# Free order for the terms of a sum, a program order chosen by replays with paused loads, paced w_ada rows, c as a column, a halved last sum

## The chip, the cores and the metric

One core of one Trainium2 chip. The metric is the device time of one execution in microseconds (us), and less is better. Before the change the median of 3 runs is 836.93 us (836.46 to 839.16).

## The reference, cut to what matters

Two decoder layers over 256 tokens of width 1024, all in fp32. Each layer is a mixing half and a SwiGLU half, and both are shifted, scaled and gated by rows of `w_ada` against silu(c).

```python
for l in range(2):
    ada = silu(c) @ w_ada[l] + b_ada[l]          # 1024 x 6144
    sh_m, sc_m, g_m, sh_f, sc_f, g_f = split(ada, 6)
    h = rms_norm(x, norm_mix[l]) * (1 + sc_m) + sh_m
    parts = h @ w_in[l]                          # 1024 x 4888 in 12 pieces
    y_a = nsa_mixer(...)                         # sparse attention, with a small MLP over key blocks
    y_b = moba_mixer(...)
    merged = gate_a * (y_a @ w_up_nsa[l]) + gate_b * (y_b @ w_up_moba[l])
    x = x + g_m * (merged @ w_out[l])
    h = rms_norm(x, norm_ffn[l]) * (1 + sc_f) + sh_f
    gt, up = split(h @ w_ffn_in[l], 2)           # 1024 x 5632
    x = x + g_f * ((silu(gt) * up) @ w_ffn_out[l])   # 2816 x 1024
```

## The kernel before, in words

Every weight is read once, in loads of about 1 MB into three buffers called `raw` (128 partitions x 2048 fp32), all from the queue of SyncE (SP, helper `dma`, L563). A loaded unit is mostly *split*: ScalarE (ACT) writes `hi`, the weight rounded to the matmul's fp32r format (L533), and VectorE (DVE) writes `lo = raw - hi` (L485). The activations are kept split in the same way (`hp` with a high and a low part, `mT`, `aT`). A product is then three matmuls into one PSUM bank: high by `hi`, high by `lo`, low by `hi`. `mm3` (L806) issues the three as one burst:

```python
with R.burst():
    mm(o, xh, wh, first, False)
    mm(o, xh, wl, False, False)
    mm(o, xl, wh, False, last)
```

`part` (L812) strings the bursts of a unit over its blocks of 128 rows. A few units are used whole in fp32 (`raw,hd` and `raw,yy` in the trace).

The order of the work on each engine is not written out by hand. The functions of the model record operations in a `Program`; `order()` lists them by a model of costs, buffers and DMA, and the result is emitted as one fixed stream for each engine. In `rounds()` the listing is repeated 40 times; `blame()` raises the rank of whatever the longest idle gaps of the matrix engine (TensorE, PE) were waiting for, and the round with the shortest planned span is kept. Writes into one bank keep the order in which they were recorded. Where the plan has PE idle for 1.4 us or more, `fill()` (L415) puts in dummy matmuls on zeros (`zb`).

The stages: `lead_in` (L1019) takes c, x, the first rows of `w_ada` (tiles `sa`) and the first 1816 columns of `w_in`, one 128-row block k at a time; `sublayer_mix` makes the other columns (`dense`), the block MLP (`mlp`, L1232), both attentions, the two up-projections and `w_out`; `h_chain` turns the new x into the next `hp`; `sublayer_ffn` (L1538) does the SwiGLU half. In the lead, c arrives as a row on one partition; two ACT and two DVE operations of 1x512 make silu(c), and four fp32 matmul passes against `ones` spread it over the partitions (`crow`).

The other rows of `w_ada` come in 80 loads of 0.5 MB into three buffers `aw`. Each is multiplied with `crow` and summed by one DVE operation (`ada_dot`, L491). `ada_pace` spreads their recording among the weight loads; the planner is free to issue them earlier or later than that.

At the end `ffn_out` of layer 1 fills four banks (2 halves of the tokens by 2 halves of the columns); the last unit's terms go round all four, each is multiplied with the gate `gbc` and added to x on DVE (`resid`), and four stores write `out`.

## Time and profile before

| | us |
|---|---|
| median of 3 runs | 836.93 (836.46 to 839.16) |
| the profiled execution | 833.42 |
| span of its trace, first to last instruction | 831.5 |
| PE busy | 810.5 (97%) |
| DVE busy | 578.0 (70%) |
| ACT busy | 419.9 (50%) |
| share of the 16 DMA engines used by loads and stores | 62.9% |

The trace is read as follows. Each engine works through its own list in the order of the program, so a waiting instruction holds up those behind it. A matmul is pipelined: its own time (0.39 us for 512 columns) is longer than the distance to the next one, so "busy" counts some waiting as work, and the distance between two starts is the better measure. A row of the timeline gives start, time, engine, line, operation and, in brackets, how long the engine had been idle and on what. The chain of waits follows back from the last instruction what released each step.

### The profile page before, as it was taken

Reading aid. Unit: us, or ns where it says so; the run is one execution under the profiler, and the core shown is the slowest. Engines: PE = TensorE matmul, PEld = TensorE weight load, DVE = VectorE, ACT = ScalarE, POOL = GpSimd, SP = SyncE. Lnnn points to the kernel's source line nnn. Section 1 sums busy time; section 2 is a strip of 40 time slices with the busy share of each in tenths; the row PEclk is TensorE's granted clock in tenths of the full one; section 3 lists DMA queues with packets and bytes.
Section 4 is the critical chain, followed back from the end, with each engine's and each line's share of the span. In section 5 each row is a group of like instructions: output and inputs, shape, how many; then the busy total and the mean of one; then the engine's idle time right before and its main releaser. Section 6 shows DMA issues by size and latency. Waiting matters only on the chain.

```text
span 831.5 us, 10528 instructions
## 1 busy us (share of the span) xinstructions
PE 810.5 (97%) x3983; PEld 612.0 (74%) x3983; DVE 578.0 (70%) x1014; ACT 419.9 (50%) x667; POOL 66.1 (8%) x69
## 2 busy tenths in 40 slices
PE   9998999999999999999999999999999999999996
PEld 4566756764768887898878877776567888889885
DVE  6878877777787776778778897866378534464443
ACT  6444465861583433444376556587457534443331
POOL 4602610000000000000000313000000000000000
PEclk9999999999999999999999999999999999999999
DMA  9987474449938899887948775540284455465531
GB/s 364 381 302 254 135 263 134 178 158 333 343 121 298 281 304 327 303 308 287 347 153 283 248 239 183 187 151 1 102 294 162 138 189 181 151 203 202 200 104 50
DMA packets 75252, 183.82 MB, mean 221 GB/s; under 512 B 4129, under 2 KB 9265, under 8 KB 75202
## 3 DMA queue, kind: packets, MB, share of 16 engines
q1 hardware_dynamic: 75154, 183.08, 62.9%
q8 instruction: 31, 0.51, 0.3%
q14 instruction: 19, 0.16, 0.1%
q0 software_dynamic: 48, 0.08, 0.0%
HBM read 182.10 MB, written 1.05 MB: 220 GB/s over the span
## 4 chain that ended last, share of the span: by engine, by line
PE 77%; DVE 8%; DMA 8%; ACT 3%; issue 2%; POOL 2%; SPq 0%; DVEq 0%; POOLq 0%; ACTq 0%
PE bank L550 72%; PE bank L555 5%; DVE lo L485 4%; DMA aw<-in_w_ada 2%; DMA raw<-in_w_in 2%; ACT hi L533 2%; DMA rows<-in_rows 1%; DVE tmp L485 1%; DMA raw<-in_w_ffn_in 1%; DMA raw<-in_w_out 1%; POOL tmp L485 1%; DVE tmp L503 1%; POOL tmp L503 1%; DVE aw L491 1%; ACT hp L533 1%
## 5 line engine op out<-in xcount | busy, mean ns | idle before, releaser
L550 PE MATMUL bank<-hi,hp 128*128 128x512 f32 (+2 forms) x1296 | 408.8, 388 | 1.5 <-DVE hp L485 0.7
L485 DVE TENSOR_TENSOR lo<-raw,hi 128x2048 fp32r<-128x2048 f32 (+2 forms) x107 | 243.0, 2286 | 122.6 <-ACT hi L533 122.4
L533 ACT ACTIVATE hi<-raw 128x2048 fp32r<-128x2048 f32 (+2 forms) x107 | 201.7, 1892 | 230.3 <-PE bank L550 173.3
L550 PEld LDWEIGHTS bank<-hi,hp 128*128 128x128 f32 x1296 | 239.3, 189 | 57.0 <-issue 6.5
L550 PE MATMUL bank<-lo,hp 128*128 128x512 f32 (+2 forms) x648 | 244.9, 378 | 4.2 <-DVE lo L485 4.0
L550 PEld LDWEIGHTS bank<-lo,hp 128*128 128x128 f32 x648 | 122.4, 189 | 29.7 <-DVE lo L485 6.9
L491 DVE SCALAR_TENSOR_TENSOR aw<-aw,crow 128x1024 f32<-128x1024 f32 x80 | 95.8, 1219 | 24.6 <-DMA aw<-in_w_ada 24.4
L550 PE MATMUL bank<-hi,aT 128*128 128x512 f32 x352 | 111.9, 392 | 0.0
L550 PEld LDWEIGHTS bank<-hi,aT 128*128 128x128 f32 x352 | 66.1, 188 | 13.4
L550 PE MATMUL bank<-lo,aT 128*128 128x512 f32 x176 | 68.6, 390 | 0.0
L550 PE MATMUL bank<-raw,yy 128*128 128x512 f32 x128 | 58.3, 598 | 0.1
L550 PE MATMUL bank<-raw,hd 128*128 128x512 f32 (+1 forms) x112 | 49.1, 568 | 0.0
L550 PE MATMUL bank<-hi,mT 128*128 128x512 f32 x128 | 43.2, 404 | 0.1
L550 PEld LDWEIGHTS bank<-raw,yy 128*128 128x128 f32 x128 | 23.2, 190 | 26.2 <-issue 23.4
L497 DVE CUSTOM_DVE_ANT_0 at<-bank,maskf 128x128 f32<-128x128 f32 (+1 forms) x96 | 29.2, 352 | 16.6 <-PE bank L555 14.9
L555 PE MATMUL bank<-ident,tmp 128*128 128x128 f32 x256 | 38.6, 282 | 1.1 <-ACT tmp L874 0.4
L555 PEld LDWEIGHTS bank<-ident,tmp 128*128 128x128 f32 x256 | 31.3, 145 | 9.8 <-issue 2.6
L550 PEld LDWEIGHTS bank<-lo,aT 128*128 128x128 f32 x176 | 33.1, 188 | 6.3
L533 ACT ACTIVATE at<-at,nb,rqa 128x128 f32<-128x128 f32 (+1 forms) x64 | 34.2, 536 | 4.4 <-DVE nb L491 4.4
L550 PEld LDWEIGHTS bank<-raw,hd 128*128 128x128 f32 x112 | 20.3, 190 | 16.2 <-issue 14.3
L485 POOL TENSOR_TENSOR tmp<-tmp,tmp 128x512 f32<-128x512 f32 (+1 forms) x9 | 11.7, 1296 | 219.1 <-DVE tmp L491 212.6
L550 PEld LDWEIGHTS bank<-hi,mT 128*128 128x128 f32 x128 | 24.0, 188 | 5.7 <-DVE mT L491 0.6
(183 smaller groups left out, 723.5 us busy)
## 6 DMA issues: line engine op xcount, KB each, us to landing
raw<-in_w_ffn_in SPq DMA_DIRECT2D x44, 1024.0 KB, 5.9
aw<-in_w_ada SPq DMA_DIRECT2D x80, 512.0 KB, 4.8
raw<-in_w_in SPq DMA_DIRECT2D x30, 1024.0 KB, 5.1
raw<-in_w_ffn_out SPq DMA_DIRECT2D x22, 1024.0 KB, 5.2
sa<-in_w_ada SPq DMA_DIRECT2D x8, 1024.0 KB, 10.6
raw<-in_w_out SPq DMA_DIRECT2D x8, 1024.0 KB, 5.6
raw<-in_w_in SPq DMA_DIRECT2D x8, 908.0 KB, 8.5
raw<-in_w_up_nsa SPq DMA_DIRECT2D x4, 1024.0 KB, 5.3
```

The source lines that it names most:

```text
L485: self._vec(engs, cols(out), True, lambda v: v.tensor_tensor(AP(out), AP(a), AP(b), op=op), [a, b], [out])
L491: lambda v: v.scalar_tensor_tensor(AP(out), AP(a), AP(s), AP(b), op0=op0, op1=op1, **{k: AP(x) for k, x in kw.items()}),
L497: lambda v: v.tensor_tensor_reduce(AP(out), AP(a), AP(b), 1.0, init, op0, op1, AP(accum)),
L503: lambda v: v.tensor_scalar(AP(out), AP(a), AP(s1), AP(s2), op0=op0, **kw),
L533: op = self.p.op({"ACT": (c, [lambda: self.nc.scalar.activation(AP(out), AP(a), func, **{k: AP(x) for k, x in kw.items()})])}, reads + lis ...
L550: op = self.p.op({"PE": (cost, [lambda: self.nc.tensor.matmul(AP(out), AP(lhsT), AP(rhs), start=start, stop=stop)])}, [lhsT, rhs], [out])
L555: self.p.op({"PE": (0.109, [lambda: self.nc.tensor.transpose(AP(out), AP(a), AP(ident))])}, [a, ident], [out])
```

## The change

1. **Terms of a sum** (`mm3`, `part`, new `term` and `Sum`): the matmuls that add into one bank no longer have an order among themselves. The planner may place each as soon as its own operands are there; the one that happens to be last closes the sum.
2. **Choosing the order** (`rounds`, new `steps` and `replay`; `blame` is gone): each of 60 listings is replayed 8 times with pauses drawn at random between loads. Waits of PE in these replays raise ranks, and the listing with the shortest mean is kept. Several costs of the model are new (issue of a load 0.43 instead of 0.07 us, doubled PE cost up to 5.4 us, slower POOL, another rule for the number of dummy matmuls).
3. **Rows of w_ada** (`paced`): an `aw` load may be issued only in its recorded turn among the SP loads; the recorded spacing is changed (`ADA_PACE`).
4. **c as a column**: the host hands c as 128x8; the silu is done on 128x8 and eight transposes of broadcast columns spread it. The first `sa` is loaded in two halves.
5. **w1 of the block MLP** is rearranged on the host, so that its load is 128 rows of 2048 contiguous values instead of 128x16 pieces of 128.
6. **The last sum**: in layer 1 the fourth bank is summed in two halves of 256 columns, one after the other; the last unit's terms get ranks by bank; the gate's operations get a rank of 100; the residual and the store of that bank are in halves too.

```diff
+    def term(self, out, lhsT, rhs, first):
+        v = out.val
+        if first:
+            v.sums, v.terms, v.gone = {}, 0, 0
+        s = v.sums.setdefault(out.part, Sum())
+        v.terms += 1
+        def go():
+            v.gone += 1
+            self.nc.tensor.matmul(AP(out), AP(lhsT), AP(rhs), start=first, stop=v.gone == v.terms)
...
-    def mm3(o, xs, wh, wl, first, last):
+    def mm3(o, xs, wh, wl, first):
         xh, xl = xs[:2]
-        with R.burst():
-            mm(o, xh, wh, first, False)
-            mm(o, xh, wl, False, False)
-            mm(o, xl, wh, False, last)
+        E_.term(o, xh, wh, first)
+        E_.term(o, xh, wl, False)
+        E_.term(o, xl, wh, False)
```

```diff
 rounds()
         for i in range(self.ROUNDS):
-            self.order()
-            if best is None or self.span < best[0] - 1e-9:
-                best = (self.span, [op.boost for op in self.ops])
-            to = self.blame()
+            steps = self.steps(self.order())
+            runs = [self.replay(steps, seed) for seed in range(self.RUNS)]
+            span = sum(r[0] for r in runs) / self.RUNS
+            if best is None or span < best[0] - 1e-9:
+                best = (span, [op.boost for op in self.ops])
             for op in self.ops:
-                op.boost += self.WEIGHT * to.get(op.no, 0.0)
+                w = sum(r[1].get(op.no, 0.0) for r in runs) / self.RUNS
+                op.boost = self.FADE * (op.boost - own[op.no]) + own[op.no] + self.WEIGHT * w
 fill()
-        cost, n = self.ZERO, int((t1 - t0 - self.IDLE) / self.ZERO)
-        if t0 < 3.0:
-            cost, n = self.FIRST_ZERO
+        cost = self.ZERO * (2 if t0 < self.COLD else 1)
+        n = int((t1 - t0 - (self.IDLE if t0 > self.START else 0.2)) / cost)
 order()
-                if "SP" in op.alts and op.no != loads[0] and self.ops[loads[0]].stage == "lead":
+                if "SP" in op.alts and op.no != loads[0] and (op.paced or self.ops[loads[0]].stage == "lead"):
                     continue
 ada_rows()
-        dma(aw, A["w_ada"][l, kind * D + k * P:kind * D + (k + 1) * P], late=ada_late)
+        dma(aw, A["w_ada"][l, kind * D + k * P:kind * D + (k + 1) * P]).paced = True
```

```diff
 lead_in()
-        for i in range(2):
-            th = temp()
-            ci = cr[:, i * 512:(i + 1) * 512]
-            act(th[0:1], ci, AF.Tanh, scale=0.5)
-            stt(th[0:1], th[0:1], 1.0, ci, ALU.add, ALU.mult)
-            b = R.val("acc")
-            mm(b, ones, th[0:1], True, True)
+        cg = R.val("ccol")
+        act(cg, cc, AF.Tanh, scale=0.5)
+        stt(cg, cg, 1.0, cc, ALU.add, ALU.mult)
+        for i in range(2):
+            b = R.val("acc")
+            with R.burst():
+                for k in range(4):
+                    tr(b[:, k * P:(k + 1) * P], cg[:, 4 * i + k:4 * i + k + 1].to_broadcast([P, P]), ident)
 sublayer_ffn()
+            parts[(NT - 1, 1)] = [(0, 256), (256, 512)]
+            keys += [(i, t, k, c, e) for t in range(NT) for c in range(2) for e in parts[(t, c)]
+                     for i in range(nu - nl, nu) for k in range(2)]
...
+            R.boost = 20.0 * (4 - 2 * t - c) - e0 / 50 if l == L - 1 and i >= nu - nl else 0.0
+            mm3(b, aT[t][kk], us[i].hi[:, k, cs_], us[i].lo[:, k, cs_], kk == 0)
```

PE's emitted instructions go from 3614 to 3644, DVE's from 916 to 926, ACT's from 559 to 547, POOL's from 74 to 80; the matmuls on `aT` go from 352 and 176 of 512 columns to 340 and 170 of 512 and 24 and 12 of 256.

**Where the change moves instructions.** First SP's queue at the end of the lead: the last block's load (128x1816), the two w1 loads of the block MLP (`in_nsa_cmp_k_w1`, `in_nsa_cmp_v_w1`), rows of `w_ada` (`aw`) and the first `dense` unit (128x4x512). Before:

```order
L563 DMA raw0_473<-in_w_in 128x1816
...
L563 DMA aw1_73<-in_w_ada 128x1024
L563 DMA aw2_74<-in_w_ada 128x1024
L563 DMA aw0_72<-in_w_ada 128x1024
L563 DMA raw1_522<-in_nsa_cmp_k_w1 128x16x128
L563 DMA raw0_528<-in_nsa_cmp_v_w1 128x16x128
L563 DMA aw1_73<-in_w_ada 128x1024
L563 DMA aw2_74<-in_w_ada 128x1024
L563 DMA raw2_555<-in_w_in 128x4x512
```

and with the change:

```order
L678 DMA raw2_485<-in_w_in 128x1816
...
L678 DMA raw2_536<-in_nsa_cmp_k_w1 128x2048
L678 DMA raw1_561<-in_nsa_cmp_v_w1 128x2048
L678 DMA raw0_582<-in_w_in 128x4x512
L678 DMA aw0_72<-in_w_ada 128x1024
L678 DMA raw1_676<-in_w_in 128x4x512
```

Five `aw` loads no longer stand ahead of the first dense unit. Further on, in layer 0's SwiGLU half, the `aw` loads stand singly or by twos and threes between weight loads where they had stood in runs of three to five; one run of five is left.

Second PE at the second unit of layer 0's `w_out`, where `hi` and `lo` are the split unit, `mT` the merged activations, and a bank is one sum. Before:

```order
L550 MATMUL bank_66<-hi_1578,mT_1597 128x512
L550 MATMUL bank_67<-hi_1609,mT_1597 128x512
L550 MATMUL bank_67<-lo_1632,mT_1597 128x512
L550 MATMUL bank_67<-hi_1609,mT_1597 128x512 x2
L550 MATMUL bank_67<-lo_1632,mT_1597 128x512
```

and with the change:

```order
L662 MATMUL bank_67<-hi_1620,mT_1595 128x512 x5
L662 MATMUL bank_66<-hi_1584,mT_1595 128x512 x2
L662 MATMUL bank_67<-hi_1620,mT_1595 128x512
L662 MATMUL bank_66<-lo_1597,mT_1595 128x512
L662 MATMUL bank_67<-hi_1620,mT_1595 128x512
L662 MATMUL bank_66<-hi_1584,mT_1595 128x512
L662 MATMUL bank_67<-lo_1639,mT_1595 128x512 x3
```

One matmul on the unit's `hi` stood ahead of the first on its `lo`; now seven do, with four of the unit before among them.

Third PE in layer 1's `w_ffn_in`, ahead of the second last block of 256 columns (`hi_5354`), with the change:

```order
L662 MATMUL bank_67<-hi_5297,hp_4627 128x256
L669 MATMUL bank_69<-ident_95,tmp_75 128x128 x4
L456 LDWEIGHTS zb_109
L456 MATMUL bank_68<-zb_109 128x512
...
L662 MATMUL bank_65<-hi_5354,hp_4627 128x256
L662 MATMUL bank_65<-lo_5373,hp_4627 128x256
```

Eleven dummy matmuls stand at the mark where rows are left out; before, none stood anywhere in layer 1's SwiGLU half. The other dummies: after the lead 11 before and 4 with the change; ahead of the first real matmul 8 before and none; at the start of layer 0's SwiGLU half 3 and at the boundary of the layers 2 before, none now. Before the x transposes 11 before, and 5 and 18 around the transposes of c now.

## Rows read from the trace of the kernel before

**Rows 1.** The page's part 1: busy time of each engine over the span.

```profile
PE 810.5 (97%) x3983; PEld 612.0 (74%) x3983; DVE 578.0 (70%) x1014; ACT 419.9 (50%) x667; POOL 66.1 (8%) x69
```

**Rows 2.** Stretches of time: busy time by engine, granted clock, DMA share, GB/s.

```profile
61.00:76.00 15.00, 10.93 (x103) 7.83 (x102) 11.73 (x24) 7.46 (x12) 2.28 (x2) 0.89 0.88 319
210.00:225.00 15.00, 13.80 (x67) 11.16 (x66) 12.79 (x13) 8.49 (x7) 1.29 (x1) 1.00 1.00 362
445.00:650.00 205.00, 203.16 (x1085) 149.00 (x1084) 150.06 (x337) 123.69 (x244) 20.62 (x12) 1.00 0.54 181
700.00:750.00 50.00, 50.00 (x236) 41.82 (x235) 24.45 (x16) 19.95 (x15) 0.00 (x0) 1.00 0.56 193
...
70.00:73.00 3.00, 2.54 (x9) 2.12 (x10) 3.00 (x3) 2.08 (x8) 0.00 (x0) 0.60 1.05 406
```

**Rows 3.** The chain of waits around 220: start, time, what, count.

```profile
216.45 8.19 PE bank L550 x36
```

**Rows 4.** Timeline of PE before the first real matmul of the lead.

```profile
11.08 2.64 PE L415 MATMUL bank<-zb 128*128 128x512 bf16 x8
13.56 2.78 PE L550 MATMUL bank<-raw,hd 128*128 128x512 f32 x7
```

**Rows 5.** Timeline of PE in the lead, block k=1.

```profile
32.56 0.50 PE L550 MATMUL bank<-lo,hp 128*128 128x512 f32 x1 [1.08 <-DVE lo L485]
```

**Rows 6.** Timeline of PE between the lead and the first dense unit.

```profile
61.34 2.54 PE L415 MATMUL bank<-zb 128*128 128x512 bf16 x11
64.86 0.23 PE L550 MATMUL bank<-zb,identb 128*128 128x128 bf16 x1 [0.98 <-DVE tmp L485]
...
70.46 0.57 PE L550 MATMUL bank<-sel,at 128*128 128x60 f32 x2 [3.09 <-ACT at L533]
```

**Rows 7.** Timeline of SP's own queue at the end of the lead.

```profile
54.41 3.99 SPq L563 DMA_DIRECT2D aw<-in_w_ada  x2
```

**Rows 8.** The chain of waits after the lead.

```profile
58.51 9.32 DMA raw<-in_w_in
```

**Rows 9.** Timelines of PE, stalls and dummies from 213 to 441.

```profile
213.92 0.50 PE L550 MATMUL bank<-lo,mT 128*128 128x512 f32 x1 [1.20 <-DVE lo L485]
...
241.97 0.82 PE L415 MATMUL bank<-zb 128*128 128x512 bf16 x3
243.24 1.27 PE L555 MATMUL bank<-ident,tmp 128*128 128x128 f32 x8 [0.45 <-ACT tmp L874]
...
247.93 0.50 PE L550 MATMUL bank<-lo,hp 128*128 128x512 f32 x1 [0.42 <-DVE lo L485]
...
319.56 0.50 PE L550 MATMUL bank<-lo,hp 128*128 128x512 f32 x1 [1.50 <-DVE lo L485]
...
432.24 0.61 PE L415 MATMUL bank<-zb 128*128 128x512 bf16 x2
...
434.25 0.73 PE L550 MATMUL bank<-hi,hp 128*128 128x512 f32 x2 [0.38 <-DVE hp L485]
...
440.32 0.40 PE L550 MATMUL bank<-lo,hp 128*128 128x280 f32 x1 [0.96 <-DVE lo L485]
```

**Rows 10.** The chain of waits ahead of the stall at 319.56.

```profile
308.14 7.91 DMA aw<-in_w_ada
```

**Rows 11.** The waits: engine, waited for, us in total, times, longest us.

```profile
DVE aw L491 <- DMA aw<-in_w_ada: 24.4, 11, 5.7
```

**Rows 12.** Timeline of PE over matmuls of 256 columns.

```profile
757.23 0.40 PE L550 MATMUL bank<-hi,hp 128*128 128x256 f32 x2
757.47 0.28 PE L550 MATMUL bank<-lo,hp 128*128 128x256 f32 x1
```

**Rows 13.** Timeline of PE, its last matmul.

```profile
824.49 0.39 PE L550 MATMUL bank<-hi,aT 128*128 128x512 f32 x1
```

**Rows 14.** Timeline of DVE, the last two groups.

```profile
822.92 2.68 DVE L485 TENSOR_TENSOR tmp<-bank,gbc 128x512 f32<-128x512 f32 x4 [8.09 <-PE bank L550]
825.52 2.48 DVE L485 TENSOR_TENSOR x<-x,tmp 128x512 f32<-128x512 f32 x4
```

More of the change, by code (lines that the diff above doesn't have):

```diff
@@ L1 @@
+import random
 from collections import deque
@@ L271, in order @@
         parts = False
+        parked, aside = {}, set()
         def place(op):
             t = 0.0
+            picks = []
+            for v in op.acc:
+                if not v.placed and v not in op.new:
+                    parked.setdefault(id(v), []).append(op)
+                    aside.add(op)
+                    return None
+            if not op.new:
+                return t, picks
             taken = {}
-            picks = []
-            if any(not v.placed for v in op.acc if v not in op.new):
-                return None
             for v in op.new:
@@ L282, in place @@
                 taken[id(k)] = i + 1
-                if len(k.queue) <= i or k.queue[i] is not v:
-                    if sum(not c.busy for s in k.slots for c in s.cells) - i <= LOOSE.get(v.name, 99):
-                        return None
+                if k.queue[i] is not v:
+                    if i == 0:
+                        parked.setdefault(id(v), []).append(op)
+                        aside.add(op)
+                    return None
                 best = None
@@ L419, in fill, with steps @@
         return t0, op
-    def blame(self):
-        to, end = {}, 0.0
-        for op in sorted((o for o in self.ops if o.placed[1] == "PE"), key=lambda o: o.placed[0]):
-            t, e, c = op.placed
-            gap, end = t - end, t + c
-            if gap < 0.25 or t < self.START:
-                continue
-            seen = set()
-            while op is not None and len(seen) < 14 and op.no not in seen:
-                seen.add(op.no)
-                to[op.no] = max(to.get(op.no, 0.0), min(gap, 3.0))
-                ready, by = max(op.waits, key=lambda w: w[0], default=(0.0, None))
-                if by is not None and by.placed[1] == "PE" and len(seen) > 1 and ready < op.placed[0] - 0.3:
+    def steps(self, out):
+        at, used, held, steps = {}, {}, {}, []
+        for i, (_, e, op) in enumerate(out):
+            deps = [at[n] for n in op.preds]
+            for v in op.new:
+                for cell in v.slot.cells:
+                    was = held.get(id(cell))
+                    if was is not None:
+                        deps += used[id(was)].values()
+                    held[id(cell)] = v
+            for v in op.acc:
+                used.setdefault(id(v), {})[e] = i
+            at[op.no] = i
+            steps.append((e, op, op.alts[e][0], [(d, 0.0 if steps[d][0] == e and not steps[d][1].bytes else
+                                                  LAT["SP"] if steps[d][1].bytes else LAT[steps[d][0]]) for d in set(deps)]))
+        return steps
@@ new lines, in replay @@
+    def replay(self, steps, seed):
+        rng = random.Random(seed)
+        free = dict.fromkeys(LAT, 0.7)
+        start, end, by = [], [], []
+        dma, table, parts, gaps = 0.0, (), False, []
+        for i, (e, op, c, deps) in enumerate(steps):
+            ready, who = 0.0, -1
+            for d, lat in deps:
+                if end[d] + lat > ready:
+                    ready, who = end[d] + lat, d
+            idle = free[e]
+            if e == "PE":
+                if op.stage != "fill" and op.parts != parts:
+                    parts = op.parts
+                    idle += self.SWITCH[2]
+                if idle < self.COLD and op.stage != "fill":
+                    c *= 2
+                if ready - idle > 0.25 and ready > self.START:
+                    gaps.append((ready - idle, i))
+            elif e == "ACT":
+                if op.loads is not None:
+                    table = op.loads
+                if op.func is not None and op.func not in table:
+                    table = next(x for x in TABLES if op.func in x)
+                    idle += 1.28
+            t = max(idle, ready)
+            start.append(t)
+            by.append(who)
+            free[e] = t + c
+            if e == "SP":
+                pause = rng.random()
+                if op.stage == "lead" or pause < 0.75:
+                    pause = 0.0
+                else:
+                    pause = 0.6 * rng.random() if pause < 0.9 else 0.6 + rng.expovariate(1.4)
+                dma = max(dma, t + c + 0.1) + op.bytes / 412e3 + pause
+                end.append(dma + 1.9)
+            else:
+                end.append(t + c + (5.1 if op.bytes else 0.0))
+        to = {}
+        for gap, i in gaps:
+            n = 0
+            while i >= 0 and n < 14:
+                no = steps[i][1].no
+                to[no] = max(to.get(no, 0.0), min(gap, 3.0))
+                j, n = by[i], n + 1
+                if j >= 0 and steps[j][0] == "PE" and n > 1 and end[j] < start[i] - 0.5:
```

211 lines of the change are left out of this document (126 added, 85 removed).

## The prediction

> **What bounds the kernel now.** I first read the page's busy times [rows 1]: PE is busy for 97% of the span, every other engine far less, so a microsecond is only won where PE waits, runs dummies or runs at half clock. Busy is not work, though. In a stretch without a wait the chain shows 36 matmuls of 512 columns in 8.19 us [rows 3], so one takes its turn every 0.2275 us, while its own row says about 0.39: a shown idle of PE therefore understates a stall by 0.16 us. Next the table by stretches [rows 2]: 700 to 750, layer 1's SwiGLU half, has PE busy all through and DMA at 0.56, nothing to win. 61 to 76 has PE busy for 10.93 of 15 us at a granted clock of 0.89. 210 to 225 has DMA at 1.00 and 1.2 us of idle PE. Then the timelines of PE, where the reader is to look for brackets and for `zb` rows [rows 4 to 6], [rows 9], and last the chain and SP's queue for what was late [rows 7, 8, 10].
>
> The plan reorders everything, so I price the places where PE loses time now, then what the new order adds. The sum is made against the profiled execution, 833.42 us (span 831.5 and 1.9 around it); that lies 3.5 under the median of the runs, 836.93, and I carry the difference over to that.
>
> **Head and lead.** The first real matmul starts at 13.56, behind eight dummies begun at 11.08 [rows 4], 2.48 us after them. The change drops those dummies, shortens silu(c) (two ACT and two DVE operations of 1x512 become one each of 128x8) and lets the first row sums start on half of the first 1 MB load. The eight added transposes replace four matmul passes. If the loads then set the start, the gain is 0; if the dummies covered all of it, 2.5, and more with the earlier c. In block k=1 PE waits 1.08+0.16 = 1.2 us for `lo` [rows 5]; the new order has five sums' terms on `hi` ahead of it. But the blocks' loads run at the same rate as before and set the end of the lead in part, so I take 2.5 for both, bounds 0.5 and 5.
>
> **After the lead.** This is the largest loss: 11 dummies, 2.54 us; a wait of 0.98; one of 3.09 [rows 6]. At 67.8 the first dense unit lands, issued at 58.51 and 9.32 us on the way [rows 8], and it was issued that late because SP had two `aw` loads in front of it, 3.99 us of its queue [rows 7], with DMA behind them at 0.88 [rows 2]. The new queue has this unit right behind the two w1 loads and ahead of five `aw` loads. Five times 0.5 MB at 319 GB/s [rows 2] is 7.8 us of transfer out of its way; of that the wait for its buffer, freed by the lead's last blocks, takes some back. PE then has dense terms on `hi`, twelve of them placed before the first on `lo`, 2.7 us of work, instead of waiting for the block MLP's chain. Of the losses 2.54+1.14+3.25 = 6.9 and the clock's (below, 1.65), 8.6 in all, four dummies and some wait for the MLP's input remain: I take 6.0, bounds 3.5 and 8.5.
>
> The granted clock is 0.60 in 70 to 73, after the idle of 3.09, and 0.89 over the 15 us [rows 2]; full being 2.4 GHz and half 1.2, 0.11 of 15 us below full means 3.3 us at half clock and 1.65 us lost. The Trainium skill (TensorE: Matmul & The Clock Gate, Part 1) says that throttled is the default and that activity releases it, so an idle matrix engine falls back to 1.2 GHz. The trace agrees here. By that rule fewer dummies in this place are a risk; it is the second rival below.
>
> **w_out and the SwiGLU half of layer 0.** At 213.92 PE waits for `lo` of a unit whose `hi` is there: 1.20+0.16 = 1.36. Three dummies (3 x 0.2275 = 0.68), 0.45+0.16 and 0.42+0.16 follow at the turn to `w_ffn_in` [rows 9]. Together 3.2. Seven matmuls on the unit's `hi` and four of the unit before now stand ahead of its first `lo`, 11 x 0.2275 = 2.5 us against one matmul's 0.23: the cover is 2.3 us longer than the wait. What is late next is the transfer itself, DMA being at 1.00 [rows 2]. I take 2.5, bounds 0.5 and 3.2.
>
> **w_ada rows.** At 319.56 PE waits 1.50+0.16 = 1.66 for a `lo` [rows 9] that stood on DVE behind a row sum waiting 7.91 us on its `aw` load [rows 10]. DVE waits 24.4 us in this way in 11 places [rows 11]; only here does it reach PE at this size. With runs of `aw` loads broken up, I take 1.5, bounds 0 and 1.7. A paced load that is not yet due costs SP nothing in the plan, but one that waits for its buffer on the chip holds the weight loads behind it: that is the third rival.
>
> **Boundary of the layers.** Two dummies (0.46), 0.38+0.16 and 0.96+0.16 [rows 9] make 2.1; no dummies there now, and terms on `hi` to fill. I take 1.6, bounds 0 and 2.1.
>
> **Layer 1's mixing half.** PE is idle for 1.84 of 205 us [rows 2], spread over small waits for POOL and ACT which a free order of terms fills only in part: 1.0, bounds -1 and 1.8.
>
> **Tail.** The last matmul starts at 824.49 [rows 13]; four products and four sums on DVE then end at 828.0 [rows 14], 3.1 us after PE. The four products begin only at 822.92, after 8.09 us of idle, and then run back to back, since the banks are finished nearly together. With the gate ranked early and the banks finished one after another, the last bank's 25 matmuls of 256 columns (0.12 each, [rows 12]) take 3.0 us, in which DVE does the other banks; behind PE's end a product and a sum of 256 columns and what DVE still has queued are left, some 1.25 us by halves of the 0.67 and 0.62 that one takes there. That is 1.85 won. Thirty-six matmuls of 0.12 for eighteen of 0.2275 cost 0.2, one more store in SP's queue 0.2 or so. Net 1.4, bounds 0.7 and 1.8.
>
> **The new dummies.** Eleven `zb` matmuls stand in layer 1's SwiGLU half, where PE now has no gap [rows 2]. They run whether needed or not: 11 x 0.2275 = 2.5 us at least; the plan leaves up to 1.2 of idle beside such a group. I take -2.7, bounds -3.7 and -2.5.
>
> The contiguous w1 loads and the changed costs I put at nothing by themselves: the transfers lie beside the lead's last matmuls; without that cover they are in the 6.0.
>
> **The sum.** 2.5 + 6.0 + 2.5 + 1.5 + 1.6 + 1.0 + 1.4 - 2.7 = 13.8. Against 833.42 that is 819.6 profiled, and against the median 836.93 it is **823.1**. All lower bounds together give 0.5+3.5+0.5+0+0-1+0.7-3.7 = 0.5, all upper ones 5+8.5+3.2+1.7+2.1+1.8+1.8-2.5 = 21.6.
>
> **The rivals.**
> - *Only the ends move.* In 200 to 445 the loads are the limit (DMA at 1.00 in 210 to 225, [rows 2]), and a stall filled with `hi` terms comes back at the next unit. Kept are 2.5 + 6.0 + 1.4 - 2.7 = 7.2: 829.7. For it: the stalls sit where loads are dense [rows 9]. Against it: DMA is at 0.56 in other stretches, so a load can be pulled forward.
> - *The clock falls after the lead all the same.* Four dummies do not cover the wait for the MLP's input, PE idles for some 3 us as at 70.46 [rows 6], and dense work again runs 3.3 us at half clock: 1.65 lost and about 1.5 more of idle, so 13.8 - 3.2 = 10.6: 826.3. It would follow from the rule of the skill's page named above. Against it: twelve dense matmuls stand ready.
> - *Slower.* Paced `aw` loads hold SP's weight loads. Each weight unit of layer 0's SwiGLU half (22 of about 1 MB) then comes late by what 319.56 shows, 1.66. The gains without the 1.5 are 12.3; it decides from the eighth such unit on, and with 15 of 22 gives 24.9 - 12.3 = 12.6 lost: 849.5. For it: DVE already waits 24.4 us for these loads [rows 11]. Against it: the new order puts them singly between weight loads.
> - *All stalls go.* Upper bounds without the most daring, some 19: 818.
> - *It does not do what it says.* The third term never was what PE waited for, since loads set the pace; gains are moved on to the next load, and the new dummies eat the tail: 836. Against it: `lo` is what PE waited for, with `hi` there [rows 9].
>
> **How the numbers follow.** The forecast of 823.1 gets 0.45, the ends alone 0.18, the clock 0.13, all stalls gone 0.11, slower 0.08, nothing 0.05. The range 812 to 831.5 holds the first four but for their tails and leaves out the last two. A measurement of this kernel can tell 0.3%, 2.5 us, from no change. Faster by more than that: 0.87, the first four. Within it 0.05, slower 0.08.
>
> **What would show it.** The first raw matmul at about 11; the first dense unit landing near 61 and its first matmul by 65; no `lo` wait over 0.5 at the second unit of `w_out`; no PE wait behind an `aw` load; eleven dummies of 2.5 us in layer 1's SwiGLU half; the last DVE sum some 1.3 us after the last matmul. Wrong would be: `DVE aw` waits grown over 24.4 with PE waiting for `lo` behind them, a clock under 0.9 after the lead, or new idle of PE in 650 to 815 beside those dummies.

## The result, and the profile after

The median after is 825.6 us (824.73 to 826.58, 4 runs), beside 836.91 us before in the same comparison (836.46 to 839.16, 4 runs): a ratio of 0.986, 95% interval 0.9839 to 0.9881. The forecast was 823.1 with a range of 812 to 831.5. So the sign and the range hold. The medians are 11.3 us apart; the two profiled executions, 833.42 and 825.58, only 7.8, because the one of before was among its quickest. (Before ran again beside the experiments: its medians there were 835.58, 836.62 and 836.07, single runs from 831.77 to 840.09.)

The page of the kernel after, part 1, against [rows 1]:

```profile
PE 807.9 (98%) x4008; PEld 611.3 (74%) x4008; DVE 580.3 (70%) x1025; ACT 410.7 (50%) x654; POOL 79.6 (10%) x75
```

PE is still what bounds the kernel. Next the table by stretches of the kernel after (us; busy time and instructions of PE, PEld, DVE, ACT, POOL; granted clock, DMA share, GB/s), against [rows 2]:

```profile
61.00:76.00 15.00, 14.45 (x127) 11.08 (x126) 14.77 (x20) 7.75 (x12) 4.47 (x2) 1.00 0.79 292
200.00:215.00 15.00, 14.49 (x65) 10.82 (x64) 13.62 (x16) 8.69 (x7) 3.28 (x1) 1.00 1.02 362
700.00:750.00 50.00, 46.43 (x234) 37.71 (x233) 27.87 (x21) 22.19 (x21) 0.00 (x0) 0.97 0.53 185
746.00:749.00 3.00, 3.00 (x8) 1.05 (x8) 3.00 (x3) 1.41 (x4) 0.00 (x0) 0.51 1.05 425
```

In 61 to 76 PE is busy for 14.45 of 15 us now, for 10.93 before. The second unit of `w_out`, in 210 to 225 before, lies in 200 to 215 now: 0.5 us of idle for 1.2, with DMA at 1.02. Both are at full clock. 700 to 750, which had no gap before, has one of 3.6 us, and right behind it three microseconds at half clock. The timeline of PE shows the places of the prediction one by one (start, duration, engine, line, operation; in brackets the idle time before it and on what):

```profile
10.05 1.86 PE L669 MATMUL bank<-ident,tmp 128*128 128x128 f32 x15 [0.95 <-DVE tmp L984]
12.36 2.88 PE L662 MATMUL bank<-raw,hd 128*128 128x512 f32 x7 [0.45 <-ACT hd L631]
...
60.76 1.03 PE L456 MATMUL bank<-zb 128*128 128x512 bf16 x4
...
64.96 3.00 PE L662 MATMUL bank<-hi,hp 128*128 128x512 f32 x12
68.08 1.66 PE L662 MATMUL bank<-lo,hp 128*128 128x512 f32 x6
...
205.46 2.12 PE L662 MATMUL bank<-hi,mT 128*128 128x512 f32 x8 [0.51 <-ACT hi L631]
232.14 1.19 PE L662 MATMUL bank<-hi,hp 128*128 128x512 f32 x4 [1.09 <-DVE hp L583]
418.91 0.50 PE L662 MATMUL bank<-hi,hp 128*128 128x512 f32 x1 [0.33 <-ACT hp L631]
...
741.77 0.60 PE L669 MATMUL bank<-ident,tmp 128*128 128x128 f32 x4
745.94 4.00 PE L456 MATMUL bank<-zb 128*128 128x512 bf16 x11 [3.57 <-ACT tmp L631]
749.59 0.47 PE L662 MATMUL bank<-hi,hp 128*128 128x256 f32 x1
...
753.24 0.86 PE L662 MATMUL bank<-hi,aT 128*128 128x512 f32 x3
...
819.01 0.28 PE L662 MATMUL bank<-hi,aT 128*128 128x256 f32 x1
```

After the lead, four dummies stand where eleven stood, twelve terms on `hi` run from 64.96, and the first one on `lo` comes at 68.08 without a wait [rows 6]. At the second unit of `w_out` the wait for `lo` of [rows 9] is gone; a wait of 0.51 for the unit's `hi` is left, and 1.09 at the turn to the SwiGLU half. But at 741.77 PE does four transposes, waits 3.57 us for ACT, and then runs the eleven late dummies: 749.59 - 741.77 = 7.8 us in which 4 transposes are done.

To see all places on one scale, I counted every matmul with the median distance between starts that its kind has in before. That work comes to about 775 us in each kernel; what the span has beyond it (waits, dummies, half clock) is lost time. By the amount of work done so far:

| us of work done | place | before | after | old block first | terms in order |
|---|---|---|---|---|---|
| 0 to 40 | head and lead | 12.69 | 11.54 | 11.55 | 11.61 |
| 40 to 80 | lead's end, block MLP | 10.93 | 5.31 | 5.25 | 13.13 |
| 80 to 160 | layer 0, attention | 2.92 | 4.08 | 4.08 | 3.14 |
| 160 to 240 | `w_out`, turn to SwiGLU | 5.86 | 2.30 | 2.03 | 4.82 |
| 240 to 360 | rest of SwiGLU, layer 0 | 2.32 | 1.16 | 1.14 | 0.06 |
| 360 to 400 | boundary of the layers | 2.34 | 1.61 | 1.61 | 1.00 |
| 400 to 600 | layer 1, mixing | 11.95 | 9.41 | 9.42 | 13.8 |
| 600 to 760 | layer 1, SwiGLU | 0.21 | 8.13 | 0.53 | 0.02 |
| 760 to 775 | tail | 7.10 | 4.94 | 4.93 | 8.16 |
| sum | | 56.3 | 48.5 | 40.5 | 55.7 |

The last two columns belong to experiments below. The change wins 16.9 us in seven places, loses 7.9 in one where before lost nothing, and 1.2 in layer 0's attention.

### The profile page after: what moved, and what is told of

It reads as the page before. It is cut to its first block, busy times and chain, and to the rows that moved or that the text cites. A ratio compares the mean times of both kernels' runs of the same rounds, so it can differ in the third digit from the quotient of the medians.

```text
span 823.8 us, 10564 instructions
## 1 busy us (share of the span) xinstructions
PE 807.9 (98%) x4008; PEld 611.3 (74%) x4008; DVE 580.3 (70%) x1025; ACT 410.7 (50%) x654; POOL 79.6 (10%) x75
## 4 chain that ended last, share of the span: by engine, by line
PE 87%; DVE 4%; ACT 2%; DMA 2%; POOL 2%; issue 1%; SPq 0%; DVEq 0%; POOLq 0%; ACTq 0%
PE bank L662 76%; PE bank L648 6%; PE bank L669 5%; DMA rows<-in_rows 1%; DVE tmp L583 1%; ACT hi L631 1%; DMA raw<-in_w_out 1%; DVE lo L583 1%; POOL tmp L601 1%; DVE tmp L601 1%; ACT hp L631 1%; PE bank L456 0%; POOL tmp L583 0%; SPq L678 0%; POOL at L1430 0%
## 5 line engine op out<-in xcount | busy, mean ns | idle before, releaser
L662 PE MATMUL bank<-hi,hp 128*128 128x512 f32 (+2 forms) x1296 | 361.1, 385 | 2.2 <-DVE hp L583 1.5
L583 DVE TENSOR_TENSOR lo<-raw,hi 128x2048 fp32r<-128x2048 f32 (+2 forms) x107 | 240.4, 2261 | 113.6 <-ACT hi L631 112.9
L662 PEld LDWEIGHTS bank<-hi,hp 128*128 128x128 f32 x1296 | 234.9, 188 | 59.5 <-issue 7.0
L662 PE MATMUL bank<-lo,hp 128*128 128x512 f32 (+2 forms) x648 | 209.9, 383 | 0.3 <-DVE lo L583 0.2
L662 PEld LDWEIGHTS bank<-lo,hp 128*128 128x128 f32 x648 | 119.7, 188 | 24.7 <-issue 2.6
L662 PE MATMUL bank<-hi,aT 128*128 128x512 f32 (+1 forms) x364 | 101.7, 387 | 0.0
L662 PE MATMUL bank<-lo,aT 128*128 128x512 f32 (+1 forms) x182 | 58.3, 385 | 0.0
L662 PE MATMUL bank<-hi,mT 128*128 128x512 f32 x128 | 39.9, 403 | 0.5 <-ACT hi L631 0.5
L595 DVE CUSTOM_DVE_ANT_0 at<-bank,maskf 128x128 f32<-128x128 f32 (+1 forms) x96 | 29.5, 352 | 11.3 <-PE bank L669 8.9
L583 DVE TENSOR_TENSOR tmp<-tmp,bank 128x512 f32<-128x512 f32 (+1 forms) x24 | 15.1, 638 | 20.5 <-PE bank L662 20.5
L947 POOL TENSOR_TENSOR r<-r,mhalf 128x4 f32<-128x4 f32 x4 | 4.1, 1027 | 254.4 <-DVE r L601 254.4
```

What stands on the lines that cost most here:

```text
L583: self._vec(engs, cols(out), True, lambda v: v.tensor_tensor(AP(out), AP(a), AP(b), op=op), [a, b], [out])
L595: lambda v: v.tensor_tensor_reduce(AP(out), AP(a), AP(b), 1.0, init, op0, op1, AP(accum)),
L662: self.nc.tensor.matmul(AP(out), AP(lhsT), AP(rhs), start=first, stop=v.gone == v.terms)
L947: E_.raw("POOL", 1.1 + 0.13 * n, lambda: nc.gpsimd.tensor_tensor(AP(r), AP(r), AP(mh), op=ALU.pow), [r, mhalf], [r])
```

## The experiments

Two theories on that place. **Dummies**: the planner put eleven dummies in, and they cost what they take. **Open sums**: since a sum's terms have no order, the sums of the last block of 512 columns stay open while the next block's terms are done; their banks come free late, the wait for ACT is real, and the dummies only fill it.

**No late dummies.** The kernel after, the same order, without the eleven:

```diff
 emit()
+            if op.stage == "fill" and t > 100.0:
+                continue
```

> The changed kernel with the same order on every engine, but without the eleven dummies in layer 1's SwiGLU half (the dummies before 100 us stay). Theory A (banks): PE would wait there in any case, because the next sum's bank is still being emptied by ACT, which does three splits first; the dummies only come on top, 4.0 us. Then PE stalls some 3.5 us from 741.8, runs at half clock after it, and the kernel gains 2.5 to 4 us over the changed kernel: 821.6 to 823. Theory B (dummies alone, as forecast): without them nothing waits there and 7.4 us come back: 818.2.

Measured: 823.41 us (822.35 to 824.88, 4 runs), ratio to before 0.9853 (0.9828 to 0.9879). That is 2.2 us less than after; the spans are 0.7 apart. The wait stays without the dummies. PE's timeline and the stretches of this kernel:

```profile
742.62 0.60 PE L671 MATMUL bank<-ident,tmp 128*128 128x128 f32 x4
746.30 0.58 PE L664 MATMUL bank<-hi,hp 128*128 128x256 f32 x1 [3.08 <-ACT tmp L633]
...
752.47 0.86 PE L664 MATMUL bank<-hi,aT 128*128 128x512 f32 x3
```

```profile
746.00:749.00 3.00, 2.70 (x12) 2.70 (x13) 3.00 (x3) 2.26 (x6) 0.00 (x0) 0.50 0.97 380
749.00:752.00 3.00, 3.00 (x16) 3.00 (x15) 2.29 (x4) 0.00 (x0) 0.00 (x0) 0.50 1.01 407
```

The real matmuls behind the wait run at 0.50 of full clock (1.2 GHz) for two stretches of 3 us. So the dummies take 3.65 us (745.94 to 749.59) and spare part of such a time; net they cost 0.7 (by the spans) to 2.2 us (by the medians). Counted in the place alone, from the four transposes to the first matmul on `aT`, it is 753.24 - 741.77 = 11.47 us in after and 752.47 - 742.62 = 9.85 here: 1.6. Theory A is right that PE waits in any case; its 2.5 to 4 us for the dummies was too much. They are not the loss; the wait is. What it waits for stands in ACT's timeline of the kernel after:

```profile
739.40 5.51 ACT L631 ACTIVATE hi<-raw 128x2048 fp32r<-128x2048 f32 x3 [5.66 <-PE bank L662]
744.82 1.61 ACT L631 ACTIVATE tmp<-bank 128x512 f32<-128x512 f32 x4
```

ACT sat 5.66 us until PE let go of a `hi` buffer, then split three units in a row, and only then emptied the banks that PE needed.

**The old block first.** If open sums are the cause, closing the last full block before the next one must end it:

```diff
 fill()
+        banks = [b for b in banks if t0 < self.START or b[0] <= t0]
 sublayer_ffn()
+                R.boost = 10.0 if l == L - 1 and c0 == DFF - 768 else 0.0
                 part(b[w, t], h[t], us[w, i], i * kt, i == 0)
+            R.boost = 0.0
```

> The changed kernel with a rank of 10 for the terms of the last 512-column block of layer 1's SwiGLU half, so that its sums are closed before the last block of 256 is begun, and with dummies only in banks that are free at the time. Theory A (sums left open hold the banks): the 3.6 us wait, the 4.0 us of dummies and the stretch at half clock all go, 7 to 8 us, 818 to 818.6. Theory B (ACT's three splits are the cause, not the open sums): ACT still does the splits first, the wait moves and at most the dummies' 4.0 come back, 821.6.

Measured: **817.74 us** (817.21 to 817.91, 4 runs), ratio to before 0.9789 (0.9768 to 0.9809), 7.9 us under after and faster than both kernels. In the table the place falls from 8.13 to 0.53 and all others stay within 0.3. ACT's timeline and the stretch of this kernel:

```profile
736.28 1.91 ACT L632 ACTIVATE hi<-raw 128x2048 fp32r<-128x2048 f32 x1
738.09 1.07 ACT L632 ACTIVATE tmp<-bank 128x512 f32<-128x512 f32 x2
```

```profile
743.00:746.00 3.00, 3.00 (x20) 2.70 (x20) 2.62 (x2) 1.03 (x2) 0.00 (x0) 1.00 0.80 311
```

One split, then the banks; PE is full at clock 1.00, and the plan holds no late dummy any more. The edit's first line only keeps dummies off banks that are still held. That it is the rank that took the wait away follows from the run before: with no late dummies at all the wait stayed. (With that first line alone the planner's order is after's without the eleven dummies, but for the places of two matmuls in layer 0's SwiGLU half; it was not run.)

**Terms in order.** The kernel after with part 1 undone (and the last sum whole, since its halves rest on part 1):

```diff
-        self.p.op({"PE": (cost, [go])}, [lhsT, rhs], [out], term=s)
+        self.p.op({"PE": (cost, [go])}, [lhsT, rhs], [out])
...
-        E_.term(o, xh, wh, first)
-        E_.term(o, xh, wl, False)
-        E_.term(o, xl, wh, False)
+        with R.burst():
+            E_.term(o, xh, wh, first)
+            E_.term(o, xh, wl, False)
+            E_.term(o, xl, wh, False)
...
-            parts[(NT - 1, 1)] = [(0, 256), (256, 512)]
```

> The changed kernel with the three terms again issued as one burst in recorded order (and the last sum whole, since halves of a bank need the free order). Theory A (free terms carry the gains at w_out, at the turn to the SwiGLU half and at the boundary, and cause the loss in layer 1): those stalls of 1 us and more are back, about 6 us, the tail's 1.4 is back, the stall of 7.4 is gone: 825.6 + 6 + 1.4 - 7.4 = 825.6, within 3. Theory B (the new planner carries the gains, free terms only harm): 818 or below.

Measured: 830.25 us (829.94 to 832.5, 5 runs), ratio 0.9945 (0.9926 to 0.9964). That is over both theories. SP's queue has the first dense unit ahead of the `aw` loads here as well; it is issued at 58.90, no earlier than before (58.51, [rows 8]) and later than in after (56.52), but it lands at 64.29 for 67.83. The kernel loses 13.13 us after the lead all the same. Its ACT, DVE and PE timelines:

```profile
64.29 1.94 ACT L631 ACTIVATE hi<-raw 128x2048 fp32r<-128x2048 f32 x1 [1.14 <-DMA raw<-in_w_in]
```

```profile
67.95 2.28 DVE L583 TENSOR_TENSOR lo<-raw,hi 128x2048 fp32r<-128x2048 f32 x1
```

```profile
71.41 1.11 PE L669 MATMUL bank<-ident,tmp 128*128 128x128 f32 x4 [2.19 <-POOL tmp L583]
72.17 0.78 PE L662 MATMUL bank<-hi,hp 128*128 128x512 f32 x1
```

The first dense matmul comes at 72.17, not at 64.96: a sum in order cannot run on `hi` while DVE makes `lo` (ready at 67.95 + 2.28 = 70.23), and here four transposes that wait 2.19 us for POOL stand ahead of it too. A unit that lands 3.5 us earlier wins nothing by itself. The loss in layer 1's SwiGLU half is not there (0.02), as open sums would have it. Of the other gains, those at the boundary (1.00 lost) and in the rest of layer 0's SwiGLU half (0.06) stay without part 1; most of the gain at `w_out` and all of it in layer 1's mixing half and the tail go.

**Before, once more.**

> The kernel before, unchanged, for a second trace: its first profiled execution was 3.5 us under the median of its runs. If the loads' timing decides (theory A), this trace has a PE stall of 2 us or more behind a load that the first does not have, in 200 to 330, where DMA is near 1.00. If it is spread (theory B), no single stall over 1 us is new.

Measured: 836.1 us (one run), span 834.1, 2.6 more than the execution that the sum was made against. PE's timeline and the chain (start, duration, step) of that run:

```profile
320.12 0.50 PE L550 MATMUL bank<-lo,hp 128*128 128x512 f32 x1 [1.34 <-DVE lo L485]
339.26 0.50 PE L550 MATMUL bank<-lo,hp 128*128 128x512 f32 x1 [1.58 <-DVE lo L485]
```

```profile
328.31 7.43 DMA aw<-in_w_ada
```

The stall that [rows 9, 10] show once comes twice here, 19 us apart; the chain has the second `aw` load. Neither theory holds as written: a stall over 1 us is new, but it is under 2 and lies behind 330. It accounts for half of the 2.6 by the count of lost time, and may be a part of why before's median lies above its profiled execution; two traces do not show more.

**Free terms alone.** Before with part 1 only, under the old way of choosing the order:

```diff
-        with R.burst():
-            mm(o, xh, wh, first, False)
-            mm(o, xh, wl, False, False)
-            mm(o, xl, wh, False, last)
+        E_.term(o, xh, wh, first)
+        E_.term(o, xh, wl, False)
+        E_.term(o, xl, wh, False)
```

> The kernel before with part 1 of the change alone: terms of a sum in any order, the old choice of the order, w_ada rows unpaced, c as a row, last sum whole. Theory A (free terms by themselves leave sums open and so make the wait in layer 1, and by themselves win the stalls after the lead, at w_out and at the boundary): eleven dummies and a wait of 3 us or more in layer 1's SwiGLU half, 7 to 8 us; after the lead, w_out and boundary together 8 to 10 us better; the waits behind w_ada rows in 300 to 340 stay; total 832 to 836 against 835.6. Theory B (the new planner makes both): no such wait, and gains under 3 us: 833 to 836 too, but with the losses of before in their old places. The trace tells the two apart, not the time.

Measured: 841.23 us (837.06 to 846.61, 10 runs), ratio 1.0052 (1.0023 to 1.0081). Its waits (engine, tile, line, what for; us in total, times, longest):

```profile
PE bank L431 <- ACT tmp L549: 3.6, 1, 3.6
```

Its ACT and PE timelines after the lead:

```profile
64.21 1.94 ACT L549 ACTIVATE hi<-raw 128x2048 fp32r<-128x2048 f32 x1 [2.20 <-DMA raw<-in_w_in]
```

```profile
66.23 2.11 PE L580 MATMUL bank<-hi,hp 128*128 128x512 f32 x8
```

The same wait of 3.6 us for ACT's `tmp` is there with part 1 alone: 7.08 us lost between 600 and 760 of work. By the same count it wins 3.3 after the lead, 2.1 at `w_out` and 1.4 in layer 1's mixing half, and gives all of it back: 7.1 in that place, 3.0 in layer 0's SwiGLU half (5.36 for 2.32), 1.2 in the tail. Theory A has the wait right and the rest too good: 5.6 us with the boundary for its 8 to 10, and 841 for its 832 to 836. After the lead this run and the one with terms in order are a pair: the first dense unit lands at the same time in both (64.21 and 64.29), and the first dense matmul comes at 66.23 with free terms, at 72.17 without. So the free terms decide that place, and what after wins there beyond this run, 2.3 us by the count, goes with its earlier load (first matmul at 64.96).

Neither half of the change wins by itself what they win together. Against before, part 1 alone stands at 1.0052, everything but part 1 and the halves of the last sum at 0.9945, all of it at 0.986. What the new choice of the order (part 2) is worth by itself was not run.

A second trace of the kernel with part 1 alone:

> The kernel before with free terms alone, once more, since its ten runs went from 837.1 to 846.6 and the trace was of the fastest. Theory A (late loads meet an order with no slack): a slower run shows PE waits of 1 us and more for lo or hi in 76 to 450 that the first trace lacks, behind w_ada or weight loads. Theory B (something of the run as a whole, such as the clock): no such waits, but a lower clock or all stages longer.

Measured: 837.96 us, span 836.2. Both traces are of executions near its quickest; what makes others of them 846 long was not caught and stays open. The mean granted clock was 0.987 and 0.989 in the two over 845 us and 0.992 to 0.998 in the four under 838; whether it fell by itself or behind waits isn't shown.

The other experiments start from the old-block-first version (817.74, their fellow below), where that loss doesn't cover anything. Each undoes one part. Before's own medians were 0.5 to 1.0 us higher beside them than beside the 817.74, and the intervals of their ratios all touch its 0.9768 to 0.9809: what is said to be slower is so by its single runs, and the sizes are good to 1 us or so.

**Unpaced rows of w_ada.**

```diff
-ADA_PACE = [(1.5, 1.5, 1.0), (0.7, 0.7, 0.3)]
+ADA_PACE = [(0.4, 2.5, 0.5), (0.0, 1.2, 0.6)]
...
-        dma(aw, A["w_ada"][l, kind * D + k * P:kind * D + (k + 1) * P]).paced = True
+        dma(aw, A["w_ada"][l, kind * D + k * P:kind * D + (k + 1) * P])
```

> The version with the old block first (817.74), without pacing: w_ada loads free to be issued out of turn, recorded spacing as before the change. Theory A (runs of w_ada loads put a row sum that waits on DVE in front of a split): DVE's waits for aw go back over 15 us, PE waits of 1.3 us or more for lo reappear in 250 to 340, 819.5 to 822. Theory B (the replays alone keep those waits off PE): 817.7 within 1.

Measured: 821.55 us (820.66 to 821.95, 4 runs), ratio 0.9815 (0.98 to 0.983): 3.8 more than with the part. But not by the stall that the theory named. The waits of this kernel and its PE timeline:

```profile
DVE aw L590 <- DMA aw<-in_w_ada: 8.9, 8, 4.2
```

```profile
406.92 0.97 PE L663 MATMUL bank<-hi,aT 128*128 128x512 f32 x3 [1.39 <-ACT aT L632]
```

DVE waits for `aw` no more than in after, where it is

```profile
DVE aw L589 <- DMA aw<-in_w_ada: 8.4, 8, 3.3
```

(after's waits; 24.4 us in 11 places before, [rows 11]), and PE waits in new places. An edit of this kind makes the search end at another order everywhere, so the 3.8 is the part plus what another order happens to be worth; the two weren't told apart.

**No pauses.** The replays are run without random pauses:

```diff
-                if op.stage == "lead" or pause < 0.75:
+                if op.stage == "lead" or pause < 9.0:
```

> The version with the old block first, its order chosen by replays without random pauses. Theory A (an order that is good with every load on time breaks where loads are late): PE waits for hi or lo of 0.5 us or more come back in 76 to 450 or 445 to 650, 819.5 to 822, and the runs spread wider. Theory B (the pauses matter little, free terms give the slack): 817.7 within 1.

Measured: 820.44 us (819.34 to 821.14, 4 runs), ratio 0.98 (0.9782 to 0.9819), 2.7 more, 2.3 of it in layer 1's mixing half by the count of lost time. A wait of 0.7 for ACT's `yy` comes twice there (574.17 and 583.00) for once in its fellow (579.43), and one for `lo` is new; its PE timeline:

```profile
470.83 0.96 PE L663 MATMUL bank<-lo,hp 128*128 128x512 f32 x3 [0.66 <-DVE lo L584]
```

By the letter this is theory A: a wait of over 0.5 for `lo`, 820.44, and runs 1.8 us apart for its fellow's 0.7. But no load is late there: ACT splits the unit at 465.48 without waiting for it, and DVE comes to its `lo` only at 468.50, behind other work of its own. And 1.8 us is no more than after's spread (824.73 to 826.58). So nothing shows that pauses guard against late loads. With both edits together:

> The version with the old block first, with neither random pauses nor paced w_ada loads. Theory A (pauses and pacing guard against the same thing, loads that come late, and either alone is enough): together gone they cost more than the sum of the two alone (2.7 + 3.8 = 6.5), over 824, and the runs spread over 3 us. Theory B (each adds its own, or the search's luck is the difference): 820 to 824 with runs within 2 us.

Measured: 822.56 us (822.37 to 822.85, 4 runs), ratio 0.9847 (0.9799 to 0.9896). A spread of 0.5 us: an order chosen without pauses and with free `aw` loads isn't a fragile one. My theory that the two guard one another falls.

**c as a row.**

```diff
-        cc = R.val("ccol")
-        dma(cc, A["c"])
+        cr = R.val("aw")[0:1]
+        dma(cr, A["c"])
...
-                for k in range(4):
-                    tr(b[:, k * P:(k + 1) * P], cg[:, 4 * i + k:4 * i + k + 1].to_broadcast([P, P]), ident)
+            mm(b, ones, th[0:1], True, True)
```

(and the silu on 1x512, the first `sa` in one load).

> The version with the old block first, with c as a row and the first w_ada load whole, as before the change. Theory A (c's column and the half load are what moved the first real matmul from 13.56 to 12.36): first real matmul at 13.4 or later, and 1.0 to 1.5 us slower, 818.7 to 819.2. Theory B (the loads' rate sets the end of the lead whatever the start): the start is later but the end of the lead is the same within 0.4, 817.7 to 818.1.

Measured: 820.51 us (819.5 to 821.86, 4 runs), ratio 0.9805 (0.9787 to 0.9823), 2.8 more; 13.7 us lost in the first 40 us of work for 11.55. Its PE timeline:

```profile
14.16 1.67 PE L457 MATMUL bank<-zb 128*128 128x512 bf16 x7
15.67 0.62 PE L663 MATMUL bank<-raw,hd 128*128 128x512 f32 x1
```

Seven dummies stand before the first real matmul at 15.67, as eight do in [rows 4]. Theory A has the direction, but the loss is over its 1.0 to 1.5, and 15.67 is later than before's own 13.56. So without part 4 the head's gain is gone; that part 4 alone, under the old choice of the order, would win it isn't shown.

**The last sum whole.**

```diff
-            parts[(NT - 1, 1)] = [(0, 256), (256, 512)]
```

> The version with the old block first (817.74) with the last bank summed whole. Theory A (the halves let DVE finish beside PE): DVE's last sum ends some 2.5 to 3 us after the last matmul instead of 1.5, and the kernel is 1.2 to 2.5 us slower: 819 to 820.2. Theory B (the gate's early rank and the banks one after another do it, the halves add nothing): 817.7 within 0.6.

Measured: 820.9 us (819.35 to 821.63, 4 runs), ratio 0.9824 (0.9782 to 0.9867), 3.2 more, 2.4 of it in the tail. Its PE and DVE timelines:

```profile
804.68 0.82 PE L457 MATMUL bank<-zb 128*128 128x512 bf16 x3
806.24 0.66 PE L670 MATMUL bank<-ident,tmp 128*128 128x128 f32 x4 [0.74 <-DVE tmp L584]
...
813.38 0.39 PE L663 MATMUL bank<-hi,aT 128*128 128x512 f32 x1
```

```profile
814.53 0.69 DVE L584 TENSOR_TENSOR x<-x,tmp 128x512 f32<-128x512 f32 x1
```

The last sum on DVE ends at 814.53 + 0.69 = 815.22, 1.45 us after the last matmul's end (813.38 + 0.39); with halves it is 1.46 in after. So the halves don't shorten the end behind PE; theory A falls. The loss lies earlier: three dummies and a wait of 0.74 stand where PE has no term left to do until the last `aT` is there. That halves leave it such terms is my reading; the order moved elsewhere too (this kernel's last term of `w_ffn_in` starts at 804.56, its fellow's at 744.15).

**w1 in pieces.** Part 5 undone; every engine's order stays the same:

```diff
-                dma(raw, A[f"nsa_cmp_{nm}_w1"][l])
+                dma(raw, A[f"nsa_cmp_{nm}_w1"][l].rearrange("(j p) h -> p j h", p=P))
```

> The version with the old block first, with the two w1 loads as 128x16 pieces of 128 values again; the order on every engine is the same. Theory A (512-byte pieces are slower on the way, and the first dense unit lies behind them): the first dense matmul is 0.5 us or more later than 64.96 and the kernel 0.5 to 2 us slower: 818.2 to 819.7. Theory B (beside the lead's last matmuls they cost nothing): 817.7 within 0.4.

Measured: 818.55 us (817.42 to 820.52, 4 runs), ratio 0.9801 (0.9758 to 0.9844): 0.8 over 817.74 with runs that overlap, so by time it's undecided. SP's queue of this kernel shows the cost, and ACT's timeline what comes of it:

```profile
50.23 0.82 SPq L679 DMA_DIRECT2D raw<-in_nsa_cmp_k_w  x1
54.09 0.71 SPq L679 DMA_DIRECT2D raw<-in_nsa_cmp_v_w  x1
```

```profile
63.41 1.92 ACT L632 ACTIVATE hi<-raw 128x2048 fp32r<-128x2048 f32 x1 [1.78 <-DMA raw<-in_w_in]
```

An issue takes 0.33 us when the load is contiguous; the dense unit's split starts at 63.41 for 61.87, and its first matmul at 65.38 for 64.96: 0.4 us, just under theory A's 0.5.

## Why the prediction was right, and the step that failed

**The new dummies: the failed step.** The prediction put the eleven `zb` matmuls at -2.7 with bounds of -3.7 and -2.5, "where PE now has no gap". The place lost 7.9 us. The dummies were 3.65 of it, longer than 11 x 0.2275 = 2.5 as the clock was at 0.51. Most of the rest is the wait of 3.57 us for ACT at 745.94, where the step had allowed 1.2 of idle beside the group. That is the prediction's own sign of being wrong, new idle of PE in 650 to 815 beside those dummies. A plan that fills a gap says that it expects one; I priced the filler and not the hole. Its cause is part 1: a sum without order may stay open, and an open sum holds its bank and its `hi` buffers. The runs show it from three sides: without dummies the wait stays, with part 1 alone it is there, with terms in order or with the old block closed first it is gone.

**After the lead (6.0).** 5.6 by the table. Right in size and by the chain named: the unit is issued at 56.52 for 58.51, its split starts at 61.81, where it landed at 67.83 before [rows 8], its matmuls begin at 64.96, under the 65 that was to show it, the clock is 1.00 in 61 to 76 and four dummies remain. The rival of the falling clock is refuted in this place. Of the two causes the free terms are the larger: 3.3 us come with part 1 alone, and none without it.

**`w_out` and the turn (2.5).** 3.6: more than I took and than the bound of 3.2. No wait for `lo` is left, which was the mechanism. Next in line is the transfer, as the prediction had it: DMA is at 1.02 in 200 to 215, and the 0.51 that is left is for a `hi` whose split waited 6.13 us for its load, by ACT's timeline of the kernel after:

```profile
203.49 1.92 ACT L631 ACTIVATE hi<-raw 128x2048 fp32r<-128x2048 f32 x1 [6.13 <-DMA raw<-in_w_out]
```

In the run without late dummies, whose order is the same, this wait is 1.51 us: that is why its span is no more than 0.7 shorter.

**w_ada rows (1.5).** 1.2 against the profiled execution. Against the second trace of before, with two such stalls, it is 2.5. No wait of PE behind `aw` is left, and DVE waits 8.4 us for 24.4 [rows 11], so the slower rival didn't come. One reading was off without changing the price: 7.91 us [rows 10] is the load's time on the way, and DVE stood idle for at most 5.7 of it [rows 11].

**Boundary (1.6)** 0.7, a wait of 0.33 at 418.91 among what is left; **layer 1's mixing half (1.0)** 2.5, over its bound of 1.8: I took the 1.84 us of shown idle for all there was, while the count finds 11.95 lost there, most of it in rows that read as busy. With part 1 alone 1.4 of the 2.5 come. **Layer 0's attention (0)** lost 1.2 that no step named; where was not followed up.

**Head and lead (2.5).** 1.2. The wait for `lo` in block k=1 [rows 5] is gone, but PE is out of the lead only 0.6 us earlier (60.76 for 61.34): the loads' rate sets that end in part, as the prediction allowed. The first raw matmul is at 12.36, not at about 11. PE waits 0.95 us for x's second half, and that stands behind POOL and DVE, whose rows come below.

**Tail (1.4).** 2.2, over its bound of 1.8. The timeline of DVE in the kernel after (the first row belongs to the last section):

```profile
7.83 1.23 DVE L589 SCALAR_TENSOR_TENSOR sa<-sa,crow 128x1024 f32<-128x1024 f32 x1
...
815.20 1.89 DVE L583 TENSOR_TENSOR tmp<-bank,gbc 128x512 f32<-128x512 f32 x3 [1.01 <-PE bank L662]
817.01 1.88 DVE L583 TENSOR_TENSOR x<-x,tmp 128x512 f32<-128x512 f32 x3
819.33 0.76 DVE L583 TENSOR_TENSOR tmp<-bank,gbc 128x256 f32<-128x256 f32 x2 [0.44 <-PE bank L662]
820.00 0.75 DVE L583 TENSOR_TENSOR x<-x,tmp 128x256 f32<-128x256 f32 x2
```

Three banks are emptied while PE works on the fourth, and the last sum ends at 820.75, 1.46 us after the last matmul's end (819.01 + 0.28; 3.1 before, [rows 13, 14]; some 1.3 forecast). The banks' order does that and not the halves, as the whole last sum showed. The 0.2 for one more store is in no run: from the last sum to the end of the span it is 3.05 us for 3.5 before.

**w1 (0).** Not quite nothing: the loads in pieces hold SP 0.9 us longer and put the first dense matmul back by 0.4.

**The sum.** 13.8 was forecast and 7.8 came, profile to profile; of the 6.0 between them the dummies' term is 5.2. Without that term 16.5 was forecast and 15.7 came, in part because misses of -1.3 to +1.5 cancel. The median looks better forecast than that (823.1 and 825.6) because I carried 3.5 us from the profiled execution over to it, and after's two agree within 0.1: before's spread may come in part from `aw` stalls, which the change takes away. No step of the sum forecast those 3.5, so the nearness of 823.1 is luck.

## What to carry to other kernels

When a planner may order the terms of a sum freely, give it a reason to close sums: an open one keeps its bank and its operands' buffers, and here one rank for the older block was worth 7.9 of 825.6 us. Read a dummy in a plan as a sign of a gap, and price what the gap waits for. And make the sum against an execution that you have placed among the runs: a stall that comes once or twice by turns moves a median.

## What the runs showed of the hardware

**POOL beside a row sum on DVE.** The same power of 128 values took 0.58 us and 1.50 us. The timeline of POOL in the kernel after:

```profile
6.22 0.58 POOL L969 TENSOR_TENSOR rx<-rx,mhalf 128x1 f32<-128x1 f32 x1 [2.26 <-DVE rx L601]
7.97 1.50 POOL L969 TENSOR_TENSOR rx<-rx,mhalf 128x1 f32<-128x1 f32 x1 [0.91 <-DVE rx L601]
```

The second began 0.14 us after DVE's row sum at 7.83, which lasts until 9.06, and ended at 9.47. In the six kernels where the row sum began first, it took 1.47 to 1.61; in the three where it began 0.1 to 0.5 us ahead of the row sum (terms in order, no pauses, last sum whole), 0.56 or 0.57, and the row sum kept its 1.22 or 1.23. The Trainium skill (SBUF — State Buffer, Who interferes with whom) says that a VectorE instruction with two SBUF inputs contends with a GpSimd one that reads SBUF. The traces agree on POOL's side; none of them shows DVE held up.

**The clock after a short wait.** After 3.1 to 3.6 us of idle in a long dense stretch the granted clock was 0.50 or 0.51 (the lower level, 1.2 GHz) in the next 3 us, whether dummies or real work stood there, and 0.50 in the 3 us after that with real work. The Trainium skill (TensorE: Matmul & The Clock Gate, Part 1) has throttled as the default and activity as what releases it, and these rows agree.

**Issues on SP.** A load of 1 MB in 128x16 pieces of 512 bytes kept SP 0.82 and 0.71 us, a contiguous one 0.33.
